# Batched product: TensorE's seven groups as a loop with fixed addresses, all engines in one hand-synchronised section

## The chip, the cores and the metric

The kernel runs on one core of a Trainium2 chip. The metric is the device time of one execution in microseconds (us); the median over several executions counts. A core has TensorE (PE, with a separate row PEld for the loading of weights), VectorE (DVE), ScalarE (ACT), GpSimd (POOL) and SyncE (SP), which here issues every transfer between HBM and the on-chip memory SBUF. Products land in PSUM, in eight banks, and ScalarE and VectorE copy them from there to SBUF.

## The reference

```python
def setup_inputs():
    batch, dim_i, dim_j, dim_k = 32, 256, 512, 384
    return {
        "x": np.random.randn(batch, dim_i, dim_j).astype(np.float32),
        "y": np.random.randn(batch, dim_j, dim_k).astype(np.float32),
    }

def reference(x: np.ndarray, y: np.ndarray) -> np.ndarray:
    return np.einsum('bij,bjk->bik', x, y).astype(np.float32)
```

There are 32 independent products of a 256 x 512 matrix by a 512 x 384 matrix, in float32. Over all of them x has 16.8 MB, y 25.2 MB and the output 12.6 MB.

## The kernel before

The 32 matrices are taken in N = 8 groups of Q = 4. Each matrix of a group sits on its own quarter of the 128 partitions (PQ = 32), so a product instruction contracts over 32 rows, and four of them, one for each matrix, stand side by side. The steps of one group n are:

- **x n** and **y n** (L84 to L100): loads of 2 MB and 3 MB, issued by SyncE. The pools hold two x buffers and two y buffers.
- **T n** (L102 to L113), on VectorE: x is rounded to float16 (one cast of 128 x 4096, called X n below) and transposed in 32 x 32 blocks into `xt_sb`. The transposed tile has two halves, e = 0 and e = 1, one for each 128 rows of the output; one transpose instruction makes one half, or a quarter in groups 6 and 7. There are three `xt_sb` buffers and one buffer `x_r` for the rounded x.
- **R n** (L115 to L119), on VectorE: y is rounded to float16 in four chunks of four contraction steps (STEP = 4). There are two `y_r` buffers.
- **M n** (L121 to L139), on TensorE: 128 products. For e = 0 and then e = 1, the 16 contraction steps t go outside and the four matrices g inside, so the four banks of a half finish together. The eight banks (e, g) are fixed for the whole program.
- **C n** (L141 to L153), on ScalarE, and **D n**, on VectorE: copies of the banks into the output tile, 32 rows at a time in groups 0 to 5 (four copies per bank) and 64 rows at a time in groups 6 and 7 (two per bank). VectorE has one bank, (1, 3), in groups 0 to 5, none in group 6 and the four with odd g in group 7. ScalarE has the rest.
- **S n** (L155 to L163): one store of 1.5 MB, issued by SyncE. There are five output buffers.

The order on each engine is the order in which the steps are called, held with `keep`, and it comes from a list written by hand:

```python
PLAN = """
x0 x1 y0
T0 x2 y1
T1 R0 M0 C0 x3 y2
T2 D0 R1 M1 C1 x4 y3
T3 D1 R2 M2 C2 x5 y4
T4 D2 R3 M3 C3 x6 y5
T5 D3 R4 M4 C4 x7 S0 S1 S2 y6
T6 D4 R5 M5 C5 y7
T7 D5 R6 M6 C6 R7 M7 C7 D7 S3 S4 S5 S6 S7
"""
```

Each engine works through its own steps of this list in that order. The waits between engines are put in by the framework from the tiles that an instruction reads and writes. T n+1 stands ahead of R n on VectorE, so x is transposed one group ahead.

Of the kernel before, what the change touches and what calls it, by code (L numbers as in the profile page):

```python
# [1 line left out]

# [4 lines left out]


MM_DT = mybir.dt.float16
F32 = mybir.dt.float32  # L10
P = 128


Q = 4
STEP = 4
O_BUFS = 5
WIDE_GROUPS = 6

PLAN = """
x0 x1 y0
T0 x2 y1
T1 R0 M0 C0 x3 y2
T2 D0 R1 M1 C1 x4 y3
T3 D1 R2 M2 C2 x5 y4
T4 D2 R3 M3 C3 x6 y5
T5 D3 R4 M4 C4 x7 S0 S1 S2 y6
T6 D4 R5 M5 C5 y7  # L30
T7 D5 R6 M6 C6 R7 M7 C7 D7 S3 S4 S5 S6 S7
"""


@with_exitstack
def kernel(
    ctx: ExitStack,
    tc: tile.TileContext,
    x: bass.AP,
    y: bass.AP,  # L40
    out: bass.AP,
):
    nc = tc.nc

    B, I, J = x.shape
    _, _, K = y.shape

    PQ = P // Q
    R = I // PQ
    T = J // PQ  # L50
    TW = T // 2
    NE = I // P
    N = B // Q

    x_pool = ctx.enter_context(tc.tile_pool(name="x_pool", bufs=2))
    y_pool = ctx.enter_context(tc.tile_pool(name="y_pool", bufs=2))
    xr_pool = ctx.enter_context(tc.tile_pool(name="xr_pool", bufs=1))
    xt_pool = ctx.enter_context(tc.tile_pool(name="xt_pool", bufs=3))
    yr_pool = ctx.enter_context(tc.tile_pool(name="yr_pool", bufs=2))
    o_pool = ctx.enter_context(tc.tile_pool(name="o_pool", bufs=O_BUFS))  # L60
    psum_pool = ctx.enter_context(
        tc.tile_pool(name="psum", bufs=1, space=bass.MemoryType.PSUM)
    )

    keep = tc.keep_in_program_order

    bank = {
        (e, g): psum_pool.tile([P, K], F32, name=f"o_ps_{e}_{g}") for e in range(NE) for g in range(Q)
    }

    x_of, y_of, xt_of, yr_of, ps_of, o_of = {}, {}, {}, {}, {}, {}

    def width(n):
        return PQ if n < WIDE_GROUPS else 2 * PQ

    def on_vector(n, e, g):
        if n < WIDE_GROUPS:  # L80
            return (e, g) == (NE - 1, Q - 1)
        return n == N - 1 and g % 2 == 1

    def load_x(n):  # L84
        x_of[n] = x_pool.tile([P, R, J], F32, name="x_sb")
        keep(
            nc.sync.dma_start(
                out=x_of[n],
                in_=x[n * Q : (n + 1) * Q].rearrange("g (p r) j -> (g p) r j", r=R),
            )  # L90
        )

    def load_y(n):
        y_of[n] = y_pool.tile([P, T, K], F32, name="y_sb")
        keep(
            nc.sync.dma_start(
                out=y_of[n],
                in_=y[n * Q : (n + 1) * Q].rearrange("g (q t) k -> (g q) t k", t=T),
            )
        )  # L100

    def transpose_x(n):  # L102


        x_r = xr_pool.tile([P, R, J], MM_DT, name="x_r")
        keep(nc.vector.tensor_copy(x_r, x_of.pop(n)))  # L106
        xt_of[n] = xt_pool.tile([P, NE, TW, P], F32, name="xt_sb")
        b = width(n) // PQ
        src = x_r.bitcast(F32).rearrange("p (b h e) (q t) -> p b e t h q", b=b, e=NE, t=TW)
        dst = xt_of[n].rearrange("p e t (h s b) -> p b e t h s", s=PQ, b=b)  # L110
        for e in range(NE):
            for c in range(b):
                keep(nc.vector.transpose(dst[:, c, e], src[:, c, e]))  # L113

    def round_y(n):  # L115
        y_sb = y_of.pop(n)
        yr_of[n] = yr_pool.tile([P, T, K], MM_DT, name="y_r")
        for a in range(0, T, STEP):
            keep(nc.vector.tensor_copy(yr_of[n][:, a : a + STEP], y_sb[:, a : a + STEP]))  # L119

    def multiply(n):  # L121
        xt = xt_of.pop(n).bitcast(MM_DT).rearrange("p e t (m c) -> p e t m c", c=2)
        y_r = yr_of.pop(n)
        o_of[n] = o_pool.tile([P, R, K], F32, name="o_sb")
        for e in range(NE):
            for g in range(Q):
                ps_of[n, e, g] = bank[e, g]
            for t in range(T):
                for g in range(Q):
                    s = slice(g * PQ, (g + 1) * PQ)  # L130
                    keep(
                        nc.tensor.matmul(  # L132
                            ps_of[n, e, g],
                            xt[s, e, t // 2, :, t % 2],
                            y_r[s, t],
                            start=(t == 0),
                            stop=(t == T - 1),
                        )
                    )  # L139

    def collect(n, vector):  # L141
        w = width(n)
        per = P // w
        copy = nc.vector.tensor_copy if vector else nc.scalar.copy
        o = o_of[n].rearrange("p (u f) k -> p u f k", u=Q // per)
        for e in range(NE):
            for g in range(Q):
                if on_vector(n, e, g) != vector:
                    continue
                ps = ps_of.pop((n, e, g))  # L150
                a = g % per * w
                for h in range(per):
                    keep(copy(o[a : a + w, g // per, h * NE + e], ps[h * w : (h + 1) * w]))  # L153

    def store(n):  # L155
        w = width(n)
        per = P // w
        dst = out[n * Q : (n + 1) * Q].rearrange("(u g) (s f) k -> (g s) u f k", g=per, s=w)
        keep(
            nc.sync.dma_start(  # L160
                out=dst, in_=o_of.pop(n).rearrange("p (u f) k -> p u f k", u=Q // per)
            )
        )  # L163

    parts = {
        "x": load_x,
        "y": load_y,
        "T": transpose_x,
        "R": round_y,
        "M": multiply,  # L170
        "C": lambda n: collect(n, False),
        "D": lambda n: collect(n, True),
        "S": store,
    }
    for step in PLAN.split():
        parts[step[0]](int(step[1:]))


# [1 line left out]
_INS = ['x', 'y']  # L180
_OUTS = [((32, 256, 384), 'float32')]


# [23 lines left out]
```

## Time and profile before

| | |
|---|---|
| time, median of 3 runs | 134.47 us (134.36 to 134.61) |
| the profiled execution's own time | 134.66 us |
| its span in the profile | 132.9 us |
| bytes read, written | 41.94 MB, 12.58 MB: 410 GB/s over the span |
| PE, PEld busy | 61.5 us (46%), 34.9 us (26%) |
| DVE busy | 96.1 us (72%) |
| ACT busy | 91.7 us (69%) |
| mean granted TensorE clock | 0.848 |

The span is what the profile sees of the program; 1.8 us of the time lie around it. "Busy" is the time with an instruction in execution. The granted clock is the share of TensorE's full clock that it was given in a stretch. In the timeline a row gives the start, the time from the start of the first to the end of the last instruction of a merged piece, the engine, the line, the operation, its tiles and the count, and in brackets the idle time before it with what ended it. A name such as `SPq` is the instruction queue of SyncE, from which transfers are issued.

### The profile page before, as it was taken

The numbers are of one execution on the slowest core, as the hardware profiler recorded it, in microseconds if no ns is written. First come the engines' busy times: TensorE is split into PE (matmuls) and PEld (weight loads), VectorE is DVE, ScalarE is ACT, GpSimd is POOL, SyncE is SP. The second block draws the span as 40 slices with busy tenths as digits, with TensorE's granted clock in tenths as the row PEclk, the third lists the DMA queues.
The fourth block names the chain that finished last, engine by engine and source line by source line (L and its number), as shares of the span: only waits on it lengthen the run. The fifth ranks groups of instructions, "written<-read, shape, count | busy, mean of one in ns | idle before, by whom it ended". The sixth has DMA issues, their size and how long they took to land.

```text
span 132.9 us, 2437 instructions
## 1 busy us (share of the span) xinstructions
PE 61.5 (46%) x1024; PEld 34.9 (26%) x1024; DVE 96.1 (72%) x92; ACT 91.7 (69%) x193; POOL 0.2 (0%) x4
## 2 busy tenths in 40 slices
PE   0000004990399129924952395329540079887100
PEld 0000002550147014612541153115320034455000
DVE  0049999699959999999997999699951090735600
ACT  3000000089999999999999999999999961998500
POOL 0000000000000000000000000000000000000000
PEclk9999999999658975797799869985999555999955
DMA  4999999999999999999999999999999999999993
GB/s 109 429 424 441 451 414 429 446 429 412 419 471 407 404 437 441 432 409 446 429 417 414 456 432 402 414 419 429 429 464 429 414 451 400 419 425 412 400 412 141
DMA packets 3723, 54.68 MB, mean 412 GB/s; under 512 B 384, under 2 KB 384, under 8 KB 896
## 3 DMA queue, kind: packets, MB, share of 16 engines
q1 hardware_dynamic: 3712, 54.53, 96.9%
q8 instruction: 8, 0.13, 0.4%
q14 instruction: 3, 0.02, 0.0%
HBM read 41.94 MB, written 12.58 MB: 410 GB/s over the span
## 4 chain that ended last, share of the span: by engine, by line
DMA 45%; DVE 19%; ACT 15%; PE 10%; issue 4%; DVEq 1%
DMA x_sb<-in_x_dram 22%; DMA y_sb<-in_y_dram 22%; ACT o_sb L153 15%; PE o_ps L132 10%; DVE xt_sb L113 6%; DVE x_r L106 5%; DVE o_sb L153 4%; DVE y_r L119 4%; DVEq L202 1%; DVEq L106 0%
## 5 line engine op out<-in xcount | busy, mean ns | idle before, releaser
L153 ACT COPY o_sb<-o_ps 32x384 f32<-32x384 f32 (+1 forms) x192 | 90.4, 471 | 32.7 <-PE o_ps L132 25.8
L132 PE MATMUL o_ps<-y_r,xt_sb 32*128 32x384 f16 x1024 | 61.5, 399 | 61.7 <-DVE y_r L119 52.3
L132 PEld LDWEIGHTS <-xt_sb 32*128 32x128 f16 x1024 | 34.9, 113 | 87.9 <-DVE y_r L119 32.8
L119 DVE CAST y_r<-y_sb 128x1536 f16<-128x1536 f32 x32 | 28.5, 953 | 10.3 <-DMA y_sb<-in_y_dram 10.2
L113 DVE STREAM_TRANSPOSE xt_sb<-x_r 128x1024 f32<-128x1024 f32 (+1 forms) x20 | 31.7, 1631 | 0.3
L106 DVE CAST x_r<-x_sb 128x4096 f16<-128x4096 f32 x8 | 18.3, 2292 | 11.1 <-DMA x_sb<-in_x_dram 11.0
L153 DVE COPY o_sb<-o_ps 32x384 f32<-32x384 f32 (+1 forms) x32 | 17.8, 556 | 7.8 <-PE o_ps L132 3.8
L153 ACT ACT_TABLE_LOAD x1 | 1.3, 1283 | 0.7 <-PEq L191 0.7
L191 POOL MEMSET const-uint8-127<- 128x1 uint8 x1 | 0.1, 103 | 0.0
L191 POOL MEMSET const-bfloat16-1.0<- 128x1 bf16 x1 | 0.1, 102 | 0.0
L191 POOL MEMSET const-float32-0.0<- 128x1 f32 x1 | 0.1, 99 | 0.2 <-issue 0.2
L191 POOL MEMSET const-float32-1.0<- 128x1 f32 x1 | 0.1, 99 | 0.0
## 6 DMA issues: line engine op xcount, KB each, us to landing
y_sb<-in_y_dram SPq DMA_DIRECT2D x8, 3072.0 KB, 21.5
x_sb<-in_x_dram SPq DMA_DIRECT2D x8, 2048.0 KB, 22.0
out_dram<-o_sb SPq DMA_DIRECT2D x8, 1536.0 KB, 25.6
```

The lines of the kernel that those rows point to most:

```text
L106: keep(nc.vector.tensor_copy(x_r, x_of.pop(n)))
L113: keep(nc.vector.transpose(dst[:, c, e], src[:, c, e]))
L119: keep(nc.vector.tensor_copy(yr_of[n][:, a : a + STEP], y_sb[:, a : a + STEP]))
L132: nc.tensor.matmul(ps_of[n, e, g], xt[s, e, t // 2, :, t % 2], y_r[s, t], start=(t == 0), stop=(t == T - 1),)
L153: keep(copy(o[a : a + w, g // per, h * NE + e], ps[h * w : (h + 1) * w]))
L191: nc = _bacc.Bacc("TRN2", target_bir_lowering=False, num_devices=1)
L202: with _tile.TileContext(nc) as tc:
```

## The change

TensorE's instructions of groups 0 to 6 become the body of a loop of seven rounds; group 7 follows the loop. So that the body can have fixed addresses, groups 0 to 6 share one `xt` buffer (group 7 has a second), and all groups share one `y_r` buffer. The kernel leaves the framework's waits aside: all engines' streams stand in one critical section, with semaphores of the kernel's own. x gets three load buffers in place of two. The order on VectorE is now a list of its own: T n follows R n-1, X stands apart from T, and X7 and T7 stand between T6 and D5. In group 6 VectorE has bank (1, 3) as in the groups before. The order of the transfers on SyncE is the same as before; x n now waits for cast n-3 in place of n-2. Each wait is written out: T n's half e waits for the last product of half e of group n-1, chunk a of R n waits for the products of half 1 of group n-1 that read that chunk, half e of M n waits for all copies that ScalarE (and, for e = 1, VectorE) makes of those banks in group n-1.

```diff
+X_BUFS = 3
+Y_BUFS = 2
...
+LOOPED = 7
+LOOP = True
+ENGINES = (PE,)
+
+
+QUEUE = "x0 x1 y0 x2 y1 x3 y2 x4 y3 x5 y4 x6 y5 x7 S0 S1 S2 y6 y7 S3 S4 S5 S6 S7"
+
+VECTOR = """
+X0 T0 R0 X1 T1 R1 X2 D0 T2 R2 X3 D1 T3 R3 X4 D2 T4 R4 X5 D3 T5 R5 X6 D4 T6
+X7 T7 D5 R6 D6 R7 D7
+"""
...
-    xt_pool = ctx.enter_context(tc.tile_pool(name="xt_pool", bufs=3))
-    yr_pool = ctx.enter_context(tc.tile_pool(name="yr_pool", bufs=2))
...
+    x_r = pool.tile([P, R, J], MM_DT, name="x_r")
+    y_r = pool.tile([P, T, K], MM_DT, name="y_r")
+
+    xt = [pool.tile([P, NE, TW, P], F32, name=f"xt_sb_{k}") for k in range(2)]
...
-        return n == N - 1 and g % 2 == 1
...
+        return g == Q - 1 and e == NE - 1 if n < N - 1 else g % 2 == 1
+
+    def done(n, e, g):
+        return NE * Q * n + Q * e + g + 1
...
+        def load_x(n):
+            if n >= X_BUFS:
+                eng.wait_ge(x_cast, n - X_BUFS + 1)
...
+        def load_y(n):
+            if n >= Y_BUFS:
+                eng.wait_ge(y_ready[NA - 1], n - Y_BUFS + 1)
...
+        def store(n):
+            eng.wait_ge(act_done[NE - 1], n + 2)
+            eng.wait_ge(vec_done, n + 2)
...
+        for n in range(N):
+            eng.wait_ge(o_out[n], 16)
...
+        def round_x(n):
+            eng.wait_ge(x_in[n], 16)
+            if n > 0:
+                eng.wait_ge(x_ready[NE - 1], n)
+            eng.tensor_copy(x_r, x_all[:, n % X_BUFS]).then_inc(x_cast, 1)
+
+        def transpose_x(n):
...
+            dst = xt[n // LOOPED].rearrange("p e t (h s b) -> p b e t h s", s=PQ, b=b)
...
+            for e in range(NE):
+                if 0 < n < LOOPED:
+                    eng.wait_ge(products, done(n - 1, e, Q - 1))
+                for c in range(b):
+                    i = eng.transpose(dst[:, c, e], src[:, c, e])
+                i.then_inc(x_ready[e], 1)
+
+        def round_y(n):
+            eng.wait_ge(y_in[n], 16)
+            for a in range(NA):
+                if n > 0:
+                    if a < NA - 1:
+                        eng.wait_ge(y_done, (NA - 1) * (n - 1) + a + 1)
+                    else:
+                        eng.wait_ge(products, done(n - 1, NE - 1, Q - 1))
+                s = slice(a * STEP, (a + 1) * STEP)
+                eng.tensor_copy(y_r[:, s], y_all[:, n % Y_BUFS, s]).then_inc(y_ready[a], 1)
...
+    def products_of(buffer, count):
+        eng = nc.tensor
+        w = xt[buffer].bitcast(MM_DT).rearrange("p e t (m c) -> p e t m c", c=2)
         for e in range(NE):
...
+            eng.wait_ge(act_done[e], count)
+            if e == NE - 1:
+                eng.wait_ge(vec_done, count)
+            eng.wait_ge(x_ready[e], count)
             for t in range(T):
+                if e == 0 and t % STEP == 0:
+                    eng.wait_ge(y_ready[t // STEP], count)
...
+    def tensor():
+        if LOOP:
+            with nc.Fori(1, LOOPED + 1, engines=ENGINES) as count:
+                products_of(0, count)
+        else:
+            for n in range(LOOPED):
+                products_of(0, n + 1)
+        for n in range(LOOPED, N):
+            products_of(1, n + 1)
+
+    with tc.tile_critical():
+        queue()
+        scalar()
+        vector()
+        tensor()
```

In the order of the changed kernel's instructions, only TensorE has the loop's branch. SyncE's first load stands behind one semaphore instruction and one branch more than before, and at the end every engine passes two branches and one exchange of semaphores more.

## The prediction

> **What bounds the kernel now.** I read the page first: span, transfers, queues.
>
> ```profile
> span 132.9 us, 2437 instructions
> ...
> DMA  4999999999999999999999999999999999999993
> ...
> q1 hardware_dynamic: 3712, 54.53, 96.9%
> q8 instruction: 8, 0.13, 0.4%
> ```
>
> The transfer engines are busy in every slice: 54.5 MB at 410 to 440 GB/s is the span. So an engine's delay costs nothing until SyncE has nothing to issue. That can only happen at the end, which I read in one-us windows (the last two columns are DMA share and GB/s), with the last store S7 from the timeline and the landing times of the stores' line:
>
> ```profile
> 126.00:127.00 1.00, 0.00 (x0) 0.00 (x0) 0.00 (x0) 0.00 (x0) 0.00 (x0) 0.76 0.90 375
> 130.00:131.00 1.00, 0.00 (x0) 0.00 (x0) 0.00 (x0) 0.00 (x0) 0.00 (x0) 0.50 0.61 252
> ...
> 125.58 0.38 SPq L160 DMA_DIRECT2D out_dram<-o_sb  x1
> ...
> DMA to landing us min/median/max: 6.5/25.6/31.0
> ```
>
> S7 is issued at 125.58, the share dips to 0.90 a microsecond later, and S7 lands after 6.5 us, the minimum: the queue had just run empty. S7 is on time with about 0.1 us to spare, so **every microsecond by which S7 is issued later is a microsecond at the end.** What S7 waits for is the last copies, so next comes VectorE's timeline:
>
> ```profile
> 20.81 3.52 DVE L119 CAST y_r<-y_sb 128x1536 f16<-128x1536 f32 x4
> ...
> 34.35 3.57 DVE L119 CAST y_r<-y_sb 128x1536 f16<-128x1536 f32 x4 [0.23 <-DMA y_sb<-in_y_dram]
> ...
> 92.42 4.06 DVE L113 STREAM_TRANSPOSE xt_sb<-x_r 128x512 f32<-128x512 f32 x4
> 97.95 2.26 DVE L153 COPY o_sb<-o_ps 32x384 f32<-32x384 f32 x4 [1.47 <-ACT o_sb L153]
> 106.21 3.56 DVE L119 CAST y_r<-y_sb 128x1536 f16<-128x1536 f32 x4 [5.99 <-DMA y_sb<-in_y_dram]
> 113.71 3.56 DVE L119 CAST y_r<-y_sb 128x1536 f16<-128x1536 f32 x4 [3.94 <-DMA y_sb<-in_y_dram]
> 119.30 2.27 DVE L153 COPY o_sb<-o_ps 64x384 f32<-64x384 f32 x4 [2.03 <-ACT o_sb L153]
> 123.25 2.27 DVE L153 COPY o_sb<-o_ps 64x384 f32<-64x384 f32 x4 [1.68 <-PE o_ps L132]
> ```
>
> These are R0, R1, T7, D5, R6, R7 and the two halves of D7. VectorE has T7 and D5 behind it at 100.2 and idles 5.99 us for y6, then 3.94 us for y7. These two reserves are what the change can use up.
>
> **The change part by part.** Names: M n.0 and M n.1 are the halves e = 0 and 1; likewise T and C.
>
> *ScalarE's pace and TensorE's halves*, from their timelines:
>
> ```profile
> 27.09 81.51 ACT L153 COPY o_sb<-o_ps 32x384 f32<-32x384 f32 x168 [25.08 <-PE o_ps L132]
> ...
> 67.91 2.78 PE L132 MATMUL o_ps<-y_r,xt_sb 32*128 32x384 f16 x62 [1.59 <-ACT o_sb L153]
> ...
> 107.23 8.67 PE L132 MATMUL o_ps<-y_r,xt_sb 32*128 32x384 f16 x131 [9.38 <-DVE y_r L119]
> ```
>
> 168 copies in 81.51 us are 0.485 each, 28 a group: 13.58 us a group without a gap, 7.76 for C n.0. A half of M takes about 2.9 us when warm. M6.0 runs from 107.23 to the first copy of C6 at 112.60: 5.37, with a granted clock of 0.51 in that stretch. After the change C0 starts about 26.9 (R0 no longer stands behind T1; y0 lands at 20.6), so C4 ends at 26.9 + 5 x 13.58 = 94.8.
>
> *VectorE's round becomes a ring with TensorE.* With one `xt`, T n+1.1 waits for M n.1; M n.1 waits for D n-1; D n-1 stands behind R n and X n+1, and R n behind T n.1. From D to D: M n.1 2.95 and latencies 0.1, half a T 1.98, R 3.60, X 2.32, D 2.30: 13.2 us, just under ScalarE's 13.58. Its start: R1 must wait for y1 at 34.35 as before, ends 37.95, X2 40.3, D0 42.6 (before, D0 was at 31.86). Four rounds later D4 ends at 42.6 + 52.8 = 95.4, later than C4. So M5.1 runs 95.4 to 98.4; before, it started at 95.07. Up to here almost nothing is lost, and M n.0, released by C n-1.0, fits between with 0.4 us or more.
>
> *The tail.* Before, T6 and T7 were ready by 96.5. Now T6.1 waits for M5.1: 98.4 + 2.05 = 100.45. X7 (2.32) ends 102.8, T7 (4.07) 106.85, D5 (2.30) 109.15, and only then comes R6: 109.15 against 106.21. VectorE's 6 us of reserve are gone and **2.9 us are lost.** Then M6.0 from the first chunk, 109.15 + 0.95 = 110.1, cold as before (the idle time before it is as long): 115.5. M6.1 2.9: 118.4. D6, now two copies on VectorE, 1.15, stands ahead of R7: 119.55. R7 had y7 at 113.71, so now D6 and the single `y_r` hold it: first chunk 120.5, last 123.15. M7.0's last 16 products take a quarter of 2.9: 123.9. C6 is through at 115.5 + 14 x 0.485 = 122.3 and doesn't hold it. M7.1: 126.8. The last half of D7, 2.27: 129.05. S7 is issued at 129.1 against 125.58: **+3.5 us** at the end. S6 needs C6, 122.3; S3 to S5 keep the transfer engines until about 124, so S6 is about on time.
>
> *Transfers.* Bytes and order stay. x n waits for an older cast than before. y6 goes out after R4: T4.1, with D3 ending near 82.2, gives R4 at 74 to 78, 1.5 us later than before, but y6 lay 29.6 us in the queue before it landed. No load starves. Cost nothing; without that cover, the same 1.5 us.
>
> *Fewer instruction packets.* q8's 0.4% of the span is 0.5 us of stream. The stream no longer sets the end, so I count nothing; if it did, -0.5.
>
> *The loop's branch.* 2048 products and weight loads came in 8 packets, so 256 a packet; a round has 256 plus a few waits, a little over one packet. A packet took 0.004 x 132.9 x 16 / 8 = 1.06 us. The nearest row for a round trip is S7: 6.5 us less 1.57 MB at 410 GB/s (3.8) is 2.7. A fetch that nothing covers would be 3.8 us, bounds 0 and 7.6 (two packets in series). TensorE has issued round n's last half about 1.5 us before it ends, and idles from M n.1's end (about 3.5 us into C n.0) to C n.0's end at 7.76: cover of 1.5 + 4.2 = 5.7 us in rounds 2 to 5, more in rounds 1 and 6. Cost 0; after the loop M7 has cover 1.5 + 2.1 us and goes straight on. [...]
>
> *The section's entry and exit.* One semaphore and branch ahead of the first load, two branches and an exchange at the end. The start's whole barrier is over at 0.73 us; VectorE's sequencer shows 0.92 us at its final branch in the chain. Bounds 0 and 2 x 0.9; I take 0.4, nearer to the start's row, where several such steps share 0.73.
>
> *TensorE's clock.* Before, M n.1 followed M n.0 within 1.6 us and ran warm. Now it waits for D, 2 to 2.6 us behind M n.0, in rounds 1 to 4. The trace grants half clock from 4 to 5 us after products end, and after that M.0 takes up to 5.37. If M n.1 starts cold or M n.0 ends before the clock rises, the ring grows by up to 2.5 us in that round. From both sides: 0, and 4 rounds x 2.5; M6.0 could also meet a warm clock earlier, -1. I take 0.8, one half-cold half with its excess partly under ScalarE's pace.
>
> **Sum**, against the profiled execution: 134.66 + 3.5 + 0.4 + 0.8 = 139.4. That execution stood 0.2 above the median of the runs: 139.2 us.
>
> **The rivals.**
> *The stream stays the bound, and it gets faster.* If the ring runs some 3.5 us ahead of my working (M5.1 ending by 95 in place of 98.4), R6 again waits for y6, S7 is again on time, and the instruction packets are saved: 134.5 - 0.5 = 134.0. For it: 97% transfer share, ScalarE and VectorE below three quarters busy. Against it: C4 can't end before 94.8, so M5.1 can't start earlier, and T6.1, X7, T7 and D5 are 10.7 us of VectorE that nothing takes from between M5.1 and R6. It decides only if D5's place or T7's wait isn't what the lists say. 6%.
> *The branch isn't covered.* Two packets in series, 7.6 us from 1.5 us before M n.1's end: M n+1.0 starts about 2 us late, less 0.4 of play, 1.6 in four rounds, and about 4 before M7: 139.2 + 6.4 + 4 = 149.6; half of that gives 144.4. It decides from a stall over 5.7 us. 12%.
> *The loop is unrolled or barriers all engines*, not what it says: the order of instructions shows a branch on TensorE alone. No chance of its own.
>
> **How the numbers follow.** My forecast has 79%, the uncovered branch 12%, the faster stream 6%, and 3% a near draw between the first and the last, with the time unchanged. About 0.2% is what a measurement of this kernel can tell from no change. So faster 0.06, same 0.03, slower 0.91. The range: low, 134.47 + 3.5 - 1 (warm clock in M6.0), and something for gaps that my row durations overstate: 136.3. High, 134.47 + 3.5 + 1.6 (section) + 4 (two rounds of cold halves less play): 143.5.
>
> **What would show it.** Right: R6 starts about 109 behind D5 and no longer waits for y6; D0 near 42; the transfer share has a gap near 128 to 130 and S7 is issued 3 to 5 us later. Branch rival: TensorE's idle time before M n.0 ends on its own sequencer, and ScalarE shows gaps once a round. Clock: M n.1 lasts over 3.5 us. Wrong altogether: R6 again ended by y6's landing.

## The result, and the profile after

The changed kernel takes 141.19 us, median of four executions (140.24 to 144.06), against 134.42 for the kernel before: a ratio of 1.0478 with an interval of 1.0416 to 1.054, slower. Executions of the changed kernel scatter over some 4 us, those of the kernel before over 0.3, and the comparisons leave out the ones that lie far above the fastest. The profiled execution took 140.24 us, the fastest of the four; against the profiled one of before (134.66) that is +5.6, and the spans differ by the same 5.6.

From the page of the changed kernel: span, busy share of the transfer engines by slice, transfer queues, and the summary of the chain that ended last (before, its first entry was DMA with 45%).

```profile
span 138.5 us, 2491 instructions
...
DMA  4999999999999999999999999999999999949164
...
q1 hardware_dynamic: 3712, 54.53, 93.1%
q8 instruction: 2, 0.03, 0.1%
...
PE 31%; DMA 23%; ACT 19%; DVE 13%; issue 8%; SPq 1%; DVEq 0%
```

The transfers are no longer the bound. The holes are all at the end; in one-us windows, with S7's issue from the timeline and the landing times of the stores' line:

```profile
123.00:124.00 1.00, 1.00 (x20) 0.37 (x24) 1.00 (x2) 0.94 (x2) 0.00 (x0) 0.69 0.12 49
128.00:129.00 1.00, 1.00 (x34) 0.59 (x24) 0.91 (x2) 0.54 (x2) 0.00 (x0) 1.00 0.64 246
130.00:131.00 1.00, 0.00 (x0) 0.00 (x0) 0.99 (x2) 0.98 (x3) 0.00 (x0) 1.00 0.00 0
132.00:133.00 1.00, 0.00 (x0) 0.00 (x0) 0.00 (x0) 0.00 (x0) 0.00 (x0) 1.00 0.46 190
...
131.73 0.38 SPq L122 DMA_DIRECT2D out_dram<-o_sb  x1
...
DMA to landing us min/median/max: 5.2/23.7/29.1
```

There are two holes (the share is the last column but one): one ahead of S6, near 124, and one ahead of S7, from 129 to 132. S7 is issued at 131.73 in place of 125.58. S6 had landed at 129.79, so S7 goes into an empty queue and lands after 5.2 us in place of 6.5.

VectorE's timeline of the changed kernel: D0, D4, D5, R6, D6, R7 and the halves of D7.

```profile
40.20 2.26 DVE L144 COPY o_sb<-o_ps 32x384 f32<-32x384 f32 x4
...
94.92 2.26 DVE L144 COPY o_sb<-o_ps 32x384 f32<-32x384 f32 x4
...
108.75 2.26 DVE L144 COPY o_sb<-o_ps 32x384 f32<-32x384 f32 x4
111.05 3.56 DVE L190 CAST y_r<-y_sb 128x1536 f16<-128x1536 f32 x4
119.87 1.12 DVE L144 COPY o_sb<-o_ps 64x384 f32<-64x384 f32 x2 [5.26 <-PE o_ps L215]
121.03 3.57 DVE L190 CAST y_r<-y_sb 128x1536 f16<-128x1536 f32 x4
126.66 2.27 DVE L144 COPY o_sb<-o_ps 64x384 f32<-64x384 f32 x4 [2.06 <-PE o_ps L215]
129.39 2.27 DVE L144 COPY o_sb<-o_ps 64x384 f32<-64x384 f32 x4 [0.46 <-PE o_ps L215]
```

R6 stands directly behind D5, with no bracket: y6 landed at 106.24, and VectorE is 4.8 us late. Before, R6 and R7 both ended waits for transfers, 5.99 and 3.94 us. Now R7 stands directly behind D6, which waits for TensorE.

TensorE's timeline, halves e = 1 of groups 1 to 4 and the whole of group 7, and the granted clock (third number from the right) in one of the halves and in M7:

```profile
42.57 2.78 PE L215 MATMUL o_ps<-y_r,xt_sb 32*128 32x384 f16 x64 [1.75 <-issue]
55.52 4.24 PE L215 MATMUL o_ps<-y_r,xt_sb 32*128 32x384 f16 x64 [2.62 <-issue]
69.94 2.78 PE L215 MATMUL o_ps<-y_r,xt_sb 32*128 32x384 f16 x64 [1.75 <-issue]
82.90 4.20 PE L215 MATMUL o_ps<-y_r,xt_sb 32*128 32x384 f16 x64 [2.69 <-issue]
122.14 7.19 PE L215 MATMUL o_ps<-y_r,xt_sb 32*128 32x384 f16 x128 [2.46 <-DVE y_r L190]
...
55.40:58.80 3.40, 3.28 (x48) 1.92 (x52) 2.05 (x2) 3.32 (x8) 0.00 (x0) 0.54 0.98 417
123.00:126.60 3.60, 3.60 (x52) 1.64 (x56) 1.60 (x2) 0.94 (x2) 0.00 (x0) 0.55 0.53 217
```

Each half starts 0.09 to 0.11 us behind the end of a D (D0 ends at 42.46, M1.1 starts at 42.57), so what the bracket calls "issue" is the wait for VectorE's copies. Of these halves every second one starts after a gap of 2.6 to 2.7 us, at half clock (0.50 granted from 55.12 to 58.53 and from 82.43 to 85.84), and takes 4.2 us in place of 2.8.

### The profile page after: what moved, and what is told of

The parts are those of the page before. It is cut to its first block, busy times and chain, and to the rows that moved or that the text cites. A ratio compares the mean times of both kernels' runs of the same rounds, so it can differ in the third digit from the quotient of the medians.

```text
span 138.5 us, 2491 instructions
## 1 busy us (share of the span) xinstructions
PE 64.2 (46%) x1024; PEld 34.9 (25%) x1024; DVE 97.1 (70%) x94; ACT 90.7 (66%) x191; POOL 0.2 (0%) x4
## 4 chain that ended last, share of the span: by engine, by line
PE 31%; DMA 23%; ACT 19%; DVE 13%; issue 8%; SPq 1%; DVEq 0%
PE o_ps L215 31%; DMA y_sb<-in_y_dram 23%; ACT o_sb L144 19%; DVE xt_sb L178 4%; DVE o_sb L144 4%; DVE y_r L190 3%; DVE x_r L165 2%; SPq L107 1%; SPq L113 0%; SPq L267 0%; DVEq L141 0%; DVEq L186 0%; DVEq L164 0%; SPq L237 0%
## 5 line engine op out<-in xcount | busy, mean ns | idle before, releaser
L144 ACT COPY o_sb<-o_ps 32x384 f32<-32x384 f32 (+1 forms) x190 | 89.4, 471 | 39.5 <-PE o_ps L215 37.2
L215 PE MATMUL o_ps<-y_r,xt_sb 32*128 32x384 f16 x1024 | 64.2, 421 | 65.2 <-DVE y_r L190 48.1
L215 PEld LDWEIGHTS o_ps<-y_r,xt_sb 32*128 32x128 f16 x1024 | 34.9, 118 | 94.0 <-issue 54.8
L178 DVE STREAM_TRANSPOSE xt_sb<-x_r 128x1024 f32<-128x1024 f32 (+1 forms) x20 | 32.4, 1643 | 9.3 <-PE o_ps L215 9.1
L144 DVE COPY o_sb<-o_ps 32x384 f32<-32x384 f32 (+1 forms) x34 | 18.9, 556 | 8.3 <-PE o_ps L215 7.8
## 6 DMA issues: line engine op xcount, KB each, us to landing
x_sb<-in_x_dram SPq DMA_DIRECT2D x8, 2048.0 KB, 23.1
```

What stands on the lines that cost most here:

```text
L144: i = copy(o[a : a + w, g // per, h * NE + e], bank[e, g][h * w : (h + 1) * w])
L178: i = eng.transpose(dst[:, c, e], src[:, c, e])
L215: i = eng.matmul(bank[e, g], w[s, e, t // 2, :, t % 2], y_r[s, t], start=(t == 0), stop=(t == T - 1),)
```

## The experiments

Theory: single buffers tie VectorE to TensorE in a ring, and with VectorE's order this uses up the reserves of the tail; the loop's branch costs nothing. Rivals: the branch, the hand-made semaphores, or the clock alone. The parts of the change were undone one or a few at a time. The times of before on the same chips are 134.4 to 134.6; ratios are against them.

**1. The loop unrolled, nothing else changed.**

```diff
-LOOP = True
+LOOP = False
```

> The changed kernel with TensorE's loop unrolled into seven copies of its body; everything else stays. Theory (the ring of single buffers and VectorE's order cost the time, the branch nothing): within 0.7 us of the changed kernel, 140.2 to 141.5 us, TensorE's halves as before, but 8 instruction packets in place of 2. Rival (the branch costs part of it): 1 to 6 us faster, 135 to 139.5, with TensorE starting its halves e = 0 earlier.

141.02 us, median of 137.18 to 142.03. The median is as the theory has it (141.19 with the loop), but the times scatter too far for a ratio, and one of the four is 3 us faster than any with the loop, as the rival would have it. The medians decide nothing here. q8 has 8 packets again. The profiled execution, 142.03 us, shows one source of the scatter:

```profile
42.46 4.46 PE L215 MATMUL o_ps<-y_r,xt_sb 32*128 32x384 f16 x64 [2.11 <-issue]
...
99.03 2.78 PE L215 MATMUL o_ps<-y_r,xt_sb 32*128 32x384 f16 x64 [1.75 <-issue]
```

It has three slow halves e = 1, M1.1, M2.1 and M4.1 (4.46, 4.35 and 4.26 us in place of 2.78), in place of two. M5.1 starts 1.74 us later than with the loop (99.03 against 97.29) and S7 is issued 1.8 later (133.5), which is the whole difference of the two profiled executions, 1.79. For the branch a sharper pair was needed, experiment 8.

**2. The section with the old buffers and the old order.**

```diff
-X_BUFS = 3
+X_BUFS = 2
-LOOP = True
+LOOP = False
+XT_BUFS = 3
+YR_BUFS = 2
-X0 T0 R0 X1 T1 R1 X2 D0 T2 R2 X3 D1 T3 R3 X4 D2 T4 R4 X5 D3 T5 R5 X6 D4 T6
-X7 T7 D5 R6 D6 R7 D7
+X0 T0 X1 T1 R0 X2 T2 D0 R1 X3 T3 D1 R2 X4 T4 D2 R3 X5 T5 D3 R4 X6 T6 D4 R5
+X7 T7 D5 R6 R7 D6 D7
...
+    def xt_of(n):
+        return n % XT_BUFS
+
+    def yr_of(n):
+        return n % YR_BUFS
```

(and each wait for a free buffer is for the last earlier group with the same buffer, in place of group n - 1)

> The hand-synchronised section kept, but unrolled, with the old buffers (three xt, two y_r, two x) and the old order of T ahead of R on VectorE; D6 stays on VectorE, behind R7. Theory (buffers and order): the transfers set the end again, R6 waits for y6 at about 106.5, and the time is that of the kernel before plus the section's entry and exit, 0.2 + 0.8: 134.6 to 135.6 us. Rival (the section's own semaphores cost the time): over 137 us.

135.31 us, ratio 1.0054 (1.0033 to 1.0075). The semaphores aren't the cost. VectorE's timeline has R6 waiting for y6 again:

```profile
106.35 3.56 DVE L203 CAST y_r<-y_sb 128x1536 f16<-128x1536 f32 x4 [6.57 <-DMA y_sb<-in_y_dram]
```

What is left over before, 0.8 us, is the section's exit: S7 lands at 132.1 in both (124.3 + 7.8 here, 125.6 + 6.5 before), and the span ends 1.6 us later here and 0.8 there.

**3. A loop with double buffers: three rounds of two groups.**

```diff
-LOOPED = 7
+LOOPED = 6
...
-            with nc.Fori(1, LOOPED + 1, engines=ENGINES) as count:
+            with nc.Fori(1, LOOPED + 1, 2, engines=ENGINES) as count:
                 products_of(0, count)
+                products_of(1, count + 1)
```

(with xt and y_r by n % 2 and the order of experiment 2)

> The loop kept, but as three rounds of two groups, so that xt and y_r have two buffers each; groups 6 and 7 behind the loop; the old order of T ahead of R on VectorE, R7 ahead of D6; three x buffers. Theory: a loop with double buffers is as fast as the unrolled one with them, 134.4 to 135.6 us, with 4 to 5 instruction packets. Rival (backward branches cost TensorE, now with a body of four packets): over 137 us, TensorE idle on its own sequencer at the start of every second group.

135.53 us, ratio 1.0077 (1.0058 to 1.0097). A loop is not slow as such; with two buffers it stands where the unrolled section stands. The page has

```profile
q8 instruction: 4, 0.07, 0.2%
```

so even a body of 512 products and weight loads, two packets and not the four of the expectation, brought no packet per round. The transfers set the end in this kernel, so a small cost of the branch would not show in its time; experiment 8 looks for that.

**4. The old order and three xt, but a single y_r.**

```diff
-LOOP = True
+LOOP = False
+XT_BUFS = 3
+YR_BUFS = 1
...
-X0 T0 R0 X1 T1 R1 X2 D0 T2 R2 X3 D1 T3 R3 X4 D2 T4 R4 X5 D3 T5 R5 X6 D4 T6
+X0 T0 X1 T1 R0 X2 T2 D0 R1 X3 T3 D1 R2 X4 T4 D2 R3 X5 T5 D3 R4 X6 T6 D4 R5
 X7 T7 D5 R6 D6 R7 D7
```

> Section kept, unrolled, three xt buffers and the old order of T ahead of R, but a single y_r as in the changed kernel (D6 ahead of R7). Theory (it is the single xt, by holding T behind the products, that starves the tail; a single y_r only puts R7 behind D6): R6 waits for y6 near 106.4, R7 starts near 117 in place of 113.8, S7 is issued near 126.3, 135.3 to 136.3 us. Rival (single y_r does as much harm as single xt): 138 us or more.

135.25 us, ratio 1.0062 (1.0046 to 1.0079). R6 waits for y6, and R7 stands behind D6:

```profile
106.32 3.57 DVE L203 CAST y_r<-y_sb 128x1536 f16<-128x1536 f32 x4 [5.74 <-DMA y_sb<-in_y_dram]
115.88 1.12 DVE L155 COPY o_sb<-o_ps 64x384 f32<-64x384 f32 x2 [5.99 <-PE o_ps L228]
117.03 3.56 DVE L203 CAST y_r<-y_sb 128x1536 f16<-128x1536 f32 x4
```

A single y_r costs R7 3.2 us (117.03 against 113.80 in experiment 2) and the kernel nothing. With three xt, the tail has room for that. With the changed order it has none, and there the single y_r does cost time (experiment 6a). Of the two single buffers, then, it is xt that starts the loss, through the order that goes with it: experiments 6b and 9 keep the single xt, change the order and lose little.

**5. The tail's order: X7 and T7 behind R6.** Loop and single buffers stay.

```diff
-X7 T7 D5 R6 D6 R7 D7
+D5 R6 X7 T7 D6 R7 D7
```

> The changed kernel, loop and single buffers kept; only X7 and T7 move behind R6 on VectorE: T6 D5 R6 X7 T7 D6 R7 D7. Theory (X7 and T7 ahead of R6 cost the tail): R6 starts near 106.5 when y6 lands, M6 near 107.5, T7 now ends near 116.5 and D6 near 117.6, so R7 starts near 117.6 in place of 121.0, S7 is issued at 127.5 to 129.3 in place of 131.7, and the time is 136 to 138.3 us. Rival (the ring before the tail is what counts, or R7 only follows T7): less than 1 us gained.

137.14 us, ratio 1.017 (1.012 to 1.022): about 4 us less than the changed kernel. R6 starts at 106.07 in place of 111.05, as soon as y6 has landed (106.04); X7 and T7 fit under M6, D6 follows at 115.97 and R7 at 117.13, as worked out. S7 goes out at 128.9: M7 took 8.26 us, where experiment 2 has 5.70. The ring was left as it was, slow halves included (M1.1, M3.1 and M5.1 took 4.2 to 4.4 us in this execution), so the clock alone does not make the loss.

**6. Group 7 with its own y_r, R7 ahead of D6**, alone (6a) and with the order of experiment 5 (6b). The last line is 6b's, the one ahead of it 6a's.

```diff
+YR_BUFS = 2
...
+    def yr_of(n):
+        return n // LOOPED
...
-X7 T7 D5 R6 D6 R7 D7
+X7 T7 D5 R6 R7 D6 D7
...
+D5 R6 X7 T7 R7 D6 D7
```

> The changed kernel with its loop and single buffers; group 7 alone gets a y_r of its own and R7 moves ahead of D6. Theory (R7 behind D6 and behind M6 costs 1 to 2 us of the tail): R7 starts near 114.7 behind R6, M7's first half no longer waits chunk by chunk, M7's second half waits for C6 near 124, S7 is issued near 129 in place of 131.7: 137 to 139 us. Rival (M7 is held by ScalarE and the clock, not by R7): within 0.7 us of the changed kernel.

138.12 us, ratio 1.0233 (1.0145 to 1.032). R7 follows R6 directly, M7 starts at 120.77 and takes 5.70 us, S7 goes out at 128.9. As expected, and about 3 us less than the changed kernel.

> Loop and single xt kept; X7 and T7 behind R6, and group 7 with a y_r of its own, R7 ahead of D6: T6 D5 R6 X7 T7 R7 D6 D7. Theory (the two reserves of the tail are given back): R6 near 106.2, R7 near 116, D6 near 119.6, M7's second half near 120.7, S7 issued near 126: at the limit of the transfers, 135.2 to 136.5 us. Rival (the ring itself costs the time, whatever the tail's order): over 137 us.

135.58 us, ratio 1.008 (1.006 to 1.01): the limit of the transfers, with the loop and the single xt still there. One execution of the four took 138.10; there is no trace of it, and its cause stays open. R6 at 106.33 waits 4.06 us for y6, R7 starts at 116.14, M7.1 at 120.91. In the other three, these two edits to a list and one more buffer undo all of the loss but the exit.

**7. The clock.** First by filling the gap between M n.0 and M n.1 with products that are thrown away, in rounds 1 to 5, unrolled:

```diff
+FILL = 10
...
+                if 1 < count < LOOPED:
+                    for _ in range(FILL):
+                        eng.matmul(bank[e, 0][:, :P], fill, fill, start=True, stop=True)
                 eng.wait_ge(vec_done, count)
```

> The changed kernel unrolled, and in rounds 1 to 5 TensorE fills the gap between its halves with ten products of a constant 128 x 128 tile into a bank that is free then and is overwritten afterwards. Theory (halves e = 1 run at half clock in some rounds because of the gap, which lengthens the ring): the granted clock stays up, every half e = 1 of rounds 1 to 5 takes 2.8 us, D4 ends 1.5 to 3 us earlier than in the unrolled kernel without filling, and the time is 138 to 140 us. Rival (the ring's excess is not the clock, or the filling delays the halves as much as it saves): 140 us or more.

140.53 us, median of 137.72 to 140.75: inconclusive. The filling had to wait for ScalarE to free the bank, so most of the gap stayed (2.27 us in round 2), and the halves behind it took

```profile
55.52 3.57 PE L222 MATMUL o_ps<-y_r,xt_sb 32*128 32x384 f16 x64
...
82.94 5.20 PE L222 MATMUL o_ps<-y_r,xt_sb 32*128 32x384 f16 x64 [0.57 <-DVE o_sb L147]
```

in place of 2.78. The filling itself took 1.25 us in rounds 2 to 4, against 0.73 in rounds 1 and 5. So the run neither kept the clock nor showed what the clock costs. Better is to take away the cause of the gap, D's place behind X:

```diff
-X0 T0 R0 X1 T1 R1 X2 D0 T2 R2 X3 D1 T3 R3 X4 D2 T4 R4 X5 D3 T5 R5 X6 D4 T6
+X0 T0 R0 X1 T1 R1 D0 X2 T2 R2 D1 X3 T3 R3 D2 X4 T4 R4 D3 X5 T5 R5 D4 X6 T6
```

> The changed kernel, loop and single buffers kept; in rounds 0 to 4 D n stands ahead of X n+2 in place of behind it. Theory (D behind X makes VectorE's ring longer than ScalarE's pace, and opens the gap in which TensorE's clock falls): M n.1 starts when ScalarE's copies of the half end, all halves e = 1 of rounds 1 to 5 take about 2.8 us, M5.1 starts near 95.3 in place of 97.3, the tail is as long as before, and the time is 138 to 139.6 us. Rival (the ring's excess comes from elsewhere, or the clock falls all the same): within 0.7 us of the changed kernel, 140.2 to 141.5.

136.95 us, ratio 1.0155 (1.0093 to 1.0217): more than expected. TensorE's halves e = 1 of rounds 1 to 5 now end a wait for ScalarE, and none takes over 2.92 us:

```profile
54.33 2.78 PE L215 MATMUL o_ps<-y_r,xt_sb 32*128 32x384 f16 x64 [1.62 <-ACT o_sb L144]
...
94.83 2.78 PE L215 MATMUL o_ps<-y_r,xt_sb 32*128 32x384 f16 x64 [1.40 <-ACT o_sb L144]
```

M5.1 starts 2.46 us earlier (94.83 against 97.29), R6 2.45 (108.60), S7 3.2 (128.55): the profiled executions differ by 3.2 (137.07 and 140.24). So the ring's excess over ScalarE's pace cost 2.5 us, and most of the rest came from M6, 6.90 in place of 7.53. The executions also scatter less, 135.89 to 137.28.

**8. The branch, in a kernel whose end it could move**: the one of experiment 7 unrolled and looped, on one chip, five executions each.

> The kernel with D n ahead of X n+2, unrolled: no branch, eight instruction packets. It runs on one chip with its loop twin, and its end is set by the ring and the tail, so a branch's cost can't hide behind the transfers. Theory (the branch costs nothing): the medians of the two within 0.5 us, both 136 to 137.3. Rival (each branch costs TensorE something): this one at least 1 us faster than the twin.

> The loop twin: the kernel with D n ahead of X n+2 and its loop of seven rounds. Theory: 136 to 137.3 us, two instruction packets, no idle time of TensorE at a round's start that doesn't end with VectorE's or ScalarE's semaphore. Rival: at least 1 us slower than the unrolled one.

136.40 us unrolled, 136.94 with the loop; ratios 1.0127 (1.0104 to 1.0151) and 1.0172 (1.0144 to 1.0201). The difference is 0.54 us, just over the limit named, and the intervals just overlap. The profiled pair shows no place for it: 137.38 unrolled and 137.18 looped, with halves of the same length in rounds 2 to 5, and TensorE's waits ended only by VectorE and ScalarE (42.1 and 22.8 us looped, 42.2 and 23.1 unrolled). A cost of the branch of up to half a microsecond stays open; several are excluded.

**9. All orders together**, loop and single xt kept: D ahead of X, X7 and T7 behind R6, group 7 with its own y_r.

> Loop and single xt kept; D n ahead of X n+2, X7 and T7 behind R6, group 7 with a y_r of its own and R7 ahead of D6. Theory: VectorE has room everywhere, the transfers set the end with the section's 0.8 us on top, and the executions no longer scatter: all within 135.2 to 135.8 us. Rival (single xt still costs): over 136 us.

135.57 us, ratio 1.0073 (1.0046 to 1.0099), executions from 135.27 to 135.94. R6 again waits for y6 (4.46 us), and the time is at the transfers' limit plus the exit. The scatter is 0.7 us; one execution lies just above the 135.2 to 135.8 expected. No version here beats the kernel before; all that reach the limit pay the exit.

## Why the prediction was right

The prediction of 139.2 us had the direction and the path right: VectorE falls behind, R6 and R7 no longer wait for transfers, and S7 goes out late. The measured 141.19 lies inside its range. That the profiled execution (140.24) is so near to the sum for it (139.4) is partly luck. S7 was issued 6.15 us later, where the sum had 3.5 and 0.8 for the clock, and a room of 1.3 us that the sum did not have took most of the difference back. Point by point:

- **S7 as the measure of the end.** Right as a measure, but S7 was 6.15 us later, more than the 3 to 5 named as the sign, and the room was misread. S7 was not on time "with about 0.1 us to spare": before, S6 landed at 128.37, 2.8 us after S7's issue, so S7's 6.5 us hold a wait for S6. Into an empty queue S7 lands after 5.2, so it could come some 1.3 us later at no cost. Experiment 4 shows most of that room: S7 is issued at 126.48, 0.9 later than before, and lands at 131.90, before at 132.06. So 6.15 less 1.3, and 0.7 for the longer exit, make the 5.6 of the span.
- **The ring.** D0 was put at 42.6 and ended at 42.46. The four rounds to D4 were put at 13.2 each; they took 12.95, 14.42, 12.96 and 14.39 (from the starts of the transposes behind each D, 42.50, 55.45, 69.87, 82.83 and 97.22). So D4 ended at 97.2 in place of 95.4: +1.8. Two halves at half clock added 2.9, and the rest of each round was a little shorter than worked out (a warm round took 12.95 for 13.2). That ScalarE's pace would put C4's end at 94.8 was right too: in experiment 7, M5.1 starts at 94.83.
- **R6 behind T6, X7, T7 and D5.** Worked out as 10.75 us from M5.1's end to R6; measured from 100.1 to 111.05. Experiments 5 and 6b confirm it: with X7 and T7 moved, R6 starts when y6 lands, at 106.07 and 106.33. y6 itself was issued 1.7 us later than before and landed no later (106.24 against 106.19), as worked out.
- **D6 and the single y_r ahead of R7.** Right in place; experiment 6a gives it about 3 us.
- **S6 "about on time".** Wrong by 1.7 us: C6 ended at 123.96 in place of 122.3, and the hole at 124 is S6's. It cost nothing beside the later S7.
- **The branch at no cost.** Right, but for another reason: the working allowed one covered fetch a round. There was none; q8 has two packets in all. The rival of the uncovered branch had nothing to stand on. A cost of up to half a microsecond stays open (experiment 8).
- **Entry and exit 0.4.** Too small: the first load is issued 0.2 later, and from S7's landing to the end it takes 1.55 us in place of 0.82. The 0.92 us of VectorE's sequencer, one of the term's bounds, are part of a DRAIN of 2.12 us at the program's end (L202), not of a branch.
- **TensorE's clock, 0.8 us.** This term was mis-sized. The working took half clock to come 4 to 5 us after products end. But the row 126:127 that it shows has a mean of 0.76, so that fall came near 126.5, 3.3 us after the last product (123.25), and in the changed kernel the falls at 55.12 and 82.43 come 2.2 us after M2.0 and M4.0 end. In the profiled execution the ring is 1.8 longer; M6 was 0.8 shorter than worked out (7.53 for 8.3); M7 ran half cold (7.19 for 6.3) and the way from R7 to S7 was 10.7 in place of 9.55, +1.15. With smaller differences S7 came 2.6 later than the 129.1 worked out without the clock. The other executions were slower still.

The rival of the faster stream needed M5.1 to end by 95; it ended at 100.1. No run here shows a packet fetched per round, neither with a body a little over 256 instructions (two packets in the whole program) nor with one a little over 512, longer than two packets (experiment 3: four).

## What to carry to other kernels

Where transfers set the time, ask of every single buffer and every place in an engine's order which reserve ahead of the last transfers it uses up; here 6 us of idle VectorE ahead of R6 and 4 ahead of R7 were the margin, with some 1.3 us of S7's own. The loop with fixed addresses was cheap here (0.54 us between the medians of experiment 8), the single buffers that it seemed to need were not: two groups a round, or a better order with a second y_r, brought all but about 1 us back (135.53 and 135.57), most of it the section's 0.8. Once a chain of waits sets the end, put the step that frees the next engine (D) ahead of the step that only prepares (X), and expect the executions to scatter (140.24 to 144.06 us here, 134.34 to 134.61 before).

## What the runs showed of the hardware

**When the clock falls.** In the profiled executions of the kernel before and of the changed one, the stretches between two changes of TensorE's granted clock are 1 to 4 times 3.41 us long. In the changed kernel the clock falls at 48.30, 55.12, 61.95, 75.60 and 82.43, among others. A gap of 2.6 us was enough there: M2.1 starts at 55.52 after one of 2.62, with 0.54 granted from 55.4 to 58.8.

What goes with the falls in these two traces is how busy TensorE was in a piece of 3.41 us, counted from one change to the next. At full clock, the 17 pieces that were busy for up to 37% were followed by half clock, and the 18 that were busy for 53% or more by full clock. At half clock, the 15 from 81% on were followed by full clock, and the 12 up to 75% by half clock. So a gap of 2.6 us and one of 1.75 us are no fair pair. In the changed kernel the piece from 51.71 to 55.12 was busy 1.19 us, 35%, and M2.1 behind it ran at half clock. In the rounds with a gap of 1.75 us, M n.0 ran at half clock from its start and the clock rose inside the gap (at 41.47, 68.78 and 96.08). In the second kernel of experiment 7, with gaps of 1.4 to 1.6 us, the halves e = 1 of rounds 2 to 5 took 2.78 us each.

**The branch.** A backward branch of TensorE over a little more than one packet of instructions, or two, brought no packet per round (2 and 4 packets in the whole program). In the changed kernel the branch's seven rows (COMPARE_BRANCH, L229) took 0.08 to 0.23 us each, 0.21 in the median.

**The scatter.** In experiment 1 the slower executions have the lower mean clock (0.813 at 137.18 us, 0.797 at 140.12, 0.788 at 141.92 and 142.03), and one slow half more (M1.1, 4.46 us in place of 2.78) goes with the profiled one. In the second kernel of experiment 7 the mean clock doesn't follow the time (0.854 at 137.07, 0.797 at 135.89). That the times at which the clock changes cause the scatter of the changed kernel is argued, not shown.
